# Attention scores from two float32r products: keys stacked as high and low parts on 128 rows, queries copied to both halves

## The chip, the cores and the metric

The kernel runs on one core of one Trainium2 chip. The metric is the device time of one execution in microseconds (us). TensorE (PE) multiplies, VectorE (DVE) and ScalarE (ACT) do element-wise work, GpSimd (POOL) helps, and SyncE (SP) issues nearly all DMAs from one queue, in order.

## The reference, cut to what matters

One backbone layer over 512 latent and 256 context tokens of width 2048: adaLN-modulated RMSNorm, one input projection split into attention heads and RWKV-7 heads, an output projection, and SwiGLU. The part that the change touches is the windowed attention:

```
q, k = axial_rope(q), axial_rope(k)                 # 16 query heads, 4 key heads, HEAD_DIM 64
s_band = where(valid, einsum(q * 64**-0.5, k in a band of up to 384 tokens), -1e30)
s_ctx  = einsum(q * 64**-0.5, k_ctx)                # 256 context keys
p      = sink_softmax(concat(s_band, s_ctx), sink)
out    = einsum(p, concat(v_band, v_ctx))
```

The other part is the modulation vector, `mod = silu(c) @ ada_w + ada_b`: 64 of its 96 columns of 128 values are made as row sums on DVE (`ada_rows`), two halves each.

## The kernel before

All tensors are held with the channels on the 128 partitions. A float32 weight product is made as three float32r products (`mm3`): the weight is split into a rounded high part (`whi`, ACT) and a rest (`wlo`, DVE), and so is the activation. The stages in order of time are:

- **Preparation of the tokens and keys** (0 to 168 us): RMSNorm, the first modulation columns, and the key tiles `psk[0..1]`, `pskc` and the first two query tiles `psk[2..3]`.
- **Query tiles 2 and 3 of head group 0, then the values** (168 to 228 us). `rotate` applies the rotary embedding on DVE (a shuffle, two products, a sum). The values need four 512 KB weights (L421). Sixteen of the modulation row sums are emitted here, four for each weight (L420).
- **Attention** (228 to 570 us): 32 units `(g, b, i)`: head group, block of 128 queries, and pair of heads. The pair's two heads lie on partitions 0 to 63 and 64 to 127 of `qT[g, i]`, their keys on the same halves of `kT[g]`. `scores(u)` makes, for either head `e`, the scores against 512 keys (first and last block) or 640 keys, in pieces of 256, 256 and 128 columns (L472), and adds the band's masks by a bf16 product with an identity (L475). Then DVE takes the maximum (L485), ACT the exponentials (L490, L492), and DVE divides (L497). `transposed(u)` turns the probabilities on PE (L506, L512) and ACT copies them out of the single PSUM buffer `pt` (L507, L513); `values_out` multiplies with the values (L524).
- **Preparation of the eight RWKV pairs** (570 to about 1020 us): key, value and partly `r` tiles, decays and the factors that are spilled to DRAM.
- **RWKV chunks and output projection** (to about 1820 us), then **SwiGLU** (to the end).

In the attention stage PE's order is written out by hand (`manual_schedule`); the other engines' order comes from a list scheduler that works with modelled times, and each engine and the SP queue then runs its list in order. In iteration `u` PE gets the transposes of unit `u` and the scores of unit `u + 2`, and between them pieces of "fill": the remaining query tiles of group 1, four `r` tiles and the two LoRA tiles (`fill_stream`, 188 steps of three products). After a finished tile the fill is withheld for `HOLD` = 3 calls. Each iteration also emits modulation row sums:

```
for u in range(len(units)):
    advance(rows, 3 if u % 2 else 2)
```

A row sum loads 512 KB into one of four buffers `raw` of pool `wp`, which the weights of `split_weight` use too, and is one pass of DVE over 128x1024 (L171). The names that the change touches are `kT`, `qT`, `q0`, `scores`, `rsqrt_newton`'s tiles, `NPR` (the number of probability buffers `pr`, two for a unit) and `rows`.

## Time and profile before

| | us |
|---|---|
| median of 3 runs | 3333.99 (3332.64 to 3337.11) |
| profiled execution: its time | 3328.19 |
| profiled execution: its span | 3326.4 |
| mean granted TensorE clock | 0.974 of 2.4 GHz |
| PE busy | 3161.6 (95%) |
| DVE busy | 1743.5 (52%) |
| ACT busy | 1161.0 (35%) |

Busy PE time is not PE at its peak: products overlap, and only the distance from one start to the next tells what one costs. An idle time is listed with what ended it ("<-DVE pr L497": the DVE instruction of line 497 that wrote `pr`).

### The profile page before, as it was taken

What the parts mean: (1) busy time and instruction counts of PE and PEld (TensorE: products, weight loads), DVE (VectorE), ACT (ScalarE), POOL (GpSimd) and SP (SyncE); (2) the same over time, 40 slices, a digit from 0 to 9 for tenths busy, and PEclk for the clock granted to TensorE, in tenths of its full rate; (3) what the DMA queues carried; (4) which work ended last, traced back from release to release, by engine and by line L of the source; (5) the groups of instructions that cost most, each with busy time, mean ns of one, the idle gap of its engine ahead of it and who ended that gap; (6) DMA issues with size and microseconds to landing.
All of it is one profiled execution on the core that took longest, in us unless ns stands there. A gap on an engine that the chain in (4) does not pass through costs nothing.

```text
span 3326.4 us, 49781 instructions
## 1 busy us (share of the span) xinstructions
PE 3161.6 (95%) x19840; PEld 2468.2 (74%) x19840; DVE 1743.5 (52%) x2906; ACT 1161.0 (35%) x2007; POOL 561.0 (17%) x597
## 2 busy tenths in 40 slices
PE   8989889989998999999997999999999999999997
PEld 4576557767775777777776788888888888888886
DVE  3377764576656777888885653323333232323233
ACT  4213333444344555555553422212221222112221
POOL 0000000253427344434433100000000000000011
PEclk9999999999999999999998999999999999999999
DMA  9675552354536345455465353322232223222232
GB/s 326 242 237 173 182 165 77 108 144 125 138 102 187 105 125 156 141 151 152 127 189 174 128 193 125 103 85 94 92 107 89 95 92 107 94 88 92 93 111 79
DMA packets 270920, 448.41 MB, mean 135 GB/s; under 512 B 109408, under 2 KB 156768, under 8 KB 270688
## 3 DMA queue, kind: packets, MB, share of 16 engines
q1 hardware_dynamic: 270688, 445.22, 42.9%
q8 instruction: 157, 2.57, 0.3%
q14 instruction: 75, 0.61, 0.1%
HBM read 383.52 MB, written 61.60 MB: 134 GB/s over the span
## 4 chain that ended last, share of the span: by engine, by line
PE 60%; DVE 4%; DMA 2%; POOL 1%; issue 1%; SPq 1%; ACT 0%; DVEq 0%; ACTq 0%; POOLq 0%
PE ps_u L114 10%; PE ps_u L113 10%; PE ps_u L110 10%; PE ps_d L113 5%; PE ps_d L110 5%; PE ps_d L114 5%; PE ps_x L852 2%; PE ps_m L982 2%; PE ps_y L863 2%; PE ps_op L110 2%; PE ps_i L901 2%; PE ps_op L114 1%; PE ps_op L113 1%; PE ps_i L907 1%; PE ps_w L971 1%; PE ps_c L1008 1%
## 5 line engine op out<-in xcount | busy, mean ns | idle before, releaser
L1264 ACT ACTIVATE whi<-raw 128x1024 fp32r<-128x1024 f32 (+1 forms) x240 | 275.0, 1146 | 1109.0 <-PE ps_u L113 603.8
L1265 DVE TENSOR_TENSOR wlo<-raw,whi 128x1024 fp32r<-128x1024 f32 (+1 forms) x238 | 317.9, 1336 | 501.2 <-ACT whi L1264 500.5
L114 PE MATMUL ps_u<-ahi,wlo 128*128 128x512 f32 x1408 | 563.0, 400 | 1.2 <-DVE wlo L1265 1.2
L113 PE MATMUL ps_u<-alo,whi 128*128 128x512 f32 x1408 | 556.1, 395 | 0.9 <-DVE alo L1280 0.9
L110 PE MATMUL ps_u<-ahi,whi 128*128 128x512 f32 x1408 | 552.6, 393 | 4.6 <-ACT whi L1264 2.9
L113 PEld LDWEIGHTS ps_u<-alo,whi 128*128 128x128 f32 x1408 | 265.0, 188 | 70.5 <-DVE alo L1280 1.6
L110 PEld LDWEIGHTS ps_u<-ahi,whi 128*128 128x128 f32 x1408 | 265.2, 188 | 69.1 <-ACT whi L1264 4.2
L114 PEld LDWEIGHTS ps_u<-ahi,wlo 128*128 128x128 f32 x1408 | 265.1, 188 | 62.9 <-DVE wlo L1265 2.0
L205 POOL TENSOR_TENSOR sq<-sq 128x512 f32<-128x512 f32 x22 | 40.8, 1855 | 1428.1 <-ACT sq L201 1427.8
L113 PE MATMUL ps_d<-glo,whi 128*128 128x512 f32 x704 | 273.3, 389 | 0.0
L110 PE MATMUL ps_d<-ghi,whi 128*128 128x512 f32 x704 | 273.3, 389 | 0.0
L114 PE MATMUL ps_d<-ghi,wlo 128*128 128x512 f32 x704 | 273.2, 389 | 0.0
L110 PE MATMUL ps_z<-hhi,whi 128*128 128x512 f32 x544 | 230.7, 424 | 7.6 <-DVE r__3128 L309 4.0
L114 PE MATMUL ps_z<-hhi,wlo 128*128 128x512 f32 x544 | 220.1, 405 | 16.8 <-DVE wlo L106 16.8
L113 PE MATMUL ps_z<-lo,whi 128*128 128x512 f32 x544 | 219.5, 403 | 0.0
L171 DVE SCALAR_TENSOR_TENSOR arow<-arow,siluB 128x1024 f32<-128x1024 f32 x128 | 156.4, 1223 | 116.2 <-DMA arow<-ada_t 115.6
L1315 DVE SCALAR_TENSOR_TENSOR x<-ps_d,modT,x 128x512 f32<-128x512 f32 x64 | 48.1, 751 | 299.8 <-PE ps_d L114 299.8
L893 POOL TENSOR_TENSOR bdB<-XY,mk 64x256 f16<-64x256 f32 x192 | 149.3, 777 | 171.7 <-DVE XY L854 156.0
L106 DVE TENSOR_TENSOR wlo<-raw,whi 128x1024 fp32r<-128x1024 f32 x80 | 106.3, 1329 | 92.3 <-ACT whi L105 92.1
L110 PEld LDWEIGHTS ps_d<-ghi,whi 128*128 128x128 f32 x704 | 132.1, 188 | 27.6
L114 PEld LDWEIGHTS ps_d<-ghi,wlo 128*128 128x128 f32 x704 | 132.1, 188 | 27.5
L113 PEld LDWEIGHTS ps_d<-glo,whi 128*128 128x128 f32 x704 | 132.1, 188 | 27.4
(624 smaller groups left out, 5770.4 us busy)
## 6 DMA issues: line engine op xcount, KB each, us to landing
raw<-w SPq DMA_DIRECT2D x176, 512.0 KB, 3.5
arow<-ada_t SPq DMA_DIRECT2D x128, 512.0 KB, 4.2
raw<-w SPq DMA_DIRECT2D x64, 704.0 KB, 4.1
raw<-w_in SPq DMA_DIRECT2D x72, 512.0 KB, 4.1
ada<-ada_w SPq DMA_DIRECT2D x64, 512.0 KB, 6.7
p1d<-pr SPq DMA_DIRECT2D x64, 256.0 KB, 2.8
XB<-bkd SPq DMA_DIRECT2D x96, 128.0 KB, 3.2
pr<-p1d SPq DMA_DIRECT2D x48, 256.0 KB, 3.2
```

The costliest lines, as they stand in the source:

```text
L106: nc.vector.tensor_tensor(lo, raw, hi.bitcast(F32), op=ALU.subtract)
L110: mm = nc.tensor.matmul(ps, lhsT=whi, rhs=hhi, start=first, stop=False)
L113: nc.tensor.matmul(ps, lhsT=whi, rhs=hlo, start=False, stop=False)
L114: nc.tensor.matmul(ps, lhsT=wlo, rhs=hhi, start=False, stop=last)
L171: nc.vector.scalar_tensor_tensor(a, a, 1.0, siluB[:, 1024 * h:1024 * h + 1024], op0=ALU.mult, op1=ALU.mult, accum_out=macc[:, j - 32, h:h ...
L852: nc.tensor.matmul(px[:, u, :], lhsT=AL[:, d, s_ + u, :], rhs=XB[:, d, s_ + u, :], start=True, stop=True)
L863: nc.tensor.matmul(py[m, u, :n], lhsT=XB[:, d, u, 64 * h:64 * h + P][:, m], rhs=GRz[h][:, d, u, :n], start=True, stop=True)
L893: nc.gpsimd.tensor_tensor(diag(B[l], h, d), ab[h][:, d], lm(l, h, d), op=ALU.mult)
L901: nc.tensor.matmul(ps[:, d, u, :], lhsT=lhs[:, d, u, :], rhs=rhs[:, d, u, :], start=True, stop=True)
L982: nc.tensor.matmul(pm[m, u, :n], lhsT=WT[e][h][:, d, u, m], rhs=YB[h][:, d, u, :n], start=True, stop=True)
L1264: nc.scalar.activation(hi[:, :n], raw[:, :n], AF.Copy)
L1265: eng.tensor_tensor(lo[:, :n], raw[:, :n], hi[:, :n].bitcast(F32), op=ALU.subtract)
```

## The change

The scores are no longer float32 products over the 64 partitions of a head. For each of the four key heads (`2 * g + e`) the keys' high part lies on partitions 0 to 63 of `KS[:, 2 * g + e]` and the keys' rest on partitions 64 to 127. The query block is copied to both halves and split into `qh` and `ql`. Two float32r products over 128 rows, `qh` and `ql` against `KS`, give the sum of all four part products. To move data between partitions, rotated keys go to DRAM (`kd_`) and come back in eight loads of 64 partitions, and rotated queries go to DRAM (`qd`) in sixteen stores and come back in two loads of 64 partitions for each unit. Keys are split once (ACT copies, DVE subtractions); queries are split for each unit (`queries`), one unit ahead of its scores. A `stage` tile takes the place of `q0` and later of the `at` pool's four `q1` tiles. `NPR` falls from 5 to 4, `rsqrt_newton`'s two scratch tiles are shared, the catch-up of the fill moves from `u == 14` to `u == 13`, and 32 of the 80 row sums of the attention loop are emitted in the preparation of the RWKV pairs.

```diff
--- before.py
+++ after.py
@@ -51,7 +51,7 @@
 NX, NM = 3, 2
 NPI, NPF = 3, 2
 POOL_LEVELS = (3, 4)
-NPR = 5
+NPR = 4
 HOLD, NE = 3, 5
 
 ORDER = "FBABAC"
@@ -115,9 +115,9 @@
 
     def rsqrt_newton(pool, x, n, lnscale, lnbias, tag):
 
-        v = pool.tile([P, n], F32, tag=tag + "v", name="rs_v", bufs=1)
+        v = pool.tile([P, T], F32, tag="rsv", name="rs_v", bufs=1)[:, :n]
         nc.scalar.activation(v, x, AF.Identity, bias=lnbias, scale=lnscale)
-        l = pool.tile([P, n], F32, tag=tag + "l", name="rs_l", bufs=1)
+        l = pool.tile([P, T], F32, tag="rsl", name="rs_l", bufs=1)[:, :n]
         nc.scalar.activation(l, v, AF.Ln)
         y = pool.tile([P, n], F32, tag=tag + "y", name="rs_y", bufs=1)
         nc.scalar.activation(y, l, AF.Exp, scale=-0.5)
@@ -224,6 +224,8 @@
     bvd = [dram.tile([P, T], F32, name=f"bvd{p}") for p in range(NP_)]
     p1d = [dram.tile([KT, P, T], F32, name=f"p1d{f}") for f in range(4)]
     gtd = [dram.tile([P, T], F32, name=f"gtd{p}") for p in range(NP_)]
+    kd_ = [dram.tile([P, TA], F32, name=f"kd{g}") for g in range(2)]
+    qd = [[dram.tile([4, 64, 2, P], F32, name=f"qd{g}_{i}") for i in range(4)] for g in range(2)]
 
     siluT = const.tile([P, KT, 32], F32, name="siluT")
     sel = const.tile([P, 2], F32, name="sel")
@@ -322,7 +324,8 @@
         kvx = ExitStack()
         kv = kvx.enter_context(tc.tile_pool(name="kv", bufs=1, reuse_waits="tile"))
         rope = kv.tile([P, 2, T], F32, name="rope")
-        kT = [kv.tile([P, TA], F32, name=f"kT{g}") for g in range(2)]
+
+        KS = kv.tile([P, 4, TA], F32R, name="KS")
         vt = kv.tile([P, 6, 256], F32, name="vt")
         shuf = [(i + 16) % 32 for i in range(32)]
 
@@ -333,13 +336,18 @@
             nc.vector.tensor_tensor(sh, sh, rope[:, 1, :], op=ALU.mult)
             nc.vector.tensor_tensor(dst, dst, sh, op=ALU.add)
 
-        qT = {}
-        q0 = zp.tile([P, 4, T], F32, tag="q0", name="q0")
+
+        stage = zp.tile([P, 4 * T], F32, tag="q0", name="stage")
         wad = []
 
+        def q_done(g, i, ps, dst):
+            rotate(ps, dst)
+            for e in range(2):
+                nc.sync.dma_start(qd[g][i][:, :, e, :].rearrange("b r x -> r b x"),
+                                  dst[64 * e:64 * e + 64].rearrange("r (b x) -> r b x", b=4))
+
         def q_tile(g, i, dst):
-            qT[g, i] = dst
-            return z_gen(T_Q + 4 * g + i, False, lambda ps, o, n: rotate(ps, qT[g, i]))
+            return z_gen(T_Q + 4 * g + i, False, lambda ps, o, n: q_done(g, i, ps, dst))
 
 
         with tc.tile_pool(name="st", bufs=2, reuse_waits="tile") as st, tc.tile_pool(name="ps_st", bufs=1, space=PSUM, reuse_waits="tile") as ps_st, \
@@ -406,13 +414,24 @@
                         w_h, w_l = (w_[:, (4 * g + i) * P:(4 * g + i + 1) * P] for w_ in w_q)
                         mm3(psk[2 + g], w_h, w_l, hhi[:, k, :], hlo[k], k == 0, k == KT - 1)
             for g in range(2):
-                rotate(psk[g], kT[g][:, C:])
-                nc.scalar.activation(kT[g][:, :C], pskc[g], AF.Copy)
+                kt = stage[:, TA * g:TA * g + TA]
+                rotate(psk[g], kt[:, C:])
+                nc.scalar.activation(kt[:, :C], pskc[g], AF.Copy)
+                nc.sync.dma_start(kd_[g], kt)
+                for e in range(2):
+                    for h in range(2):
+                        nc.sync.dma_start(KS[64 * h:64 * h + 64, 2 * g + e, :].bitcast(F32), kd_[g][64 * e:64 * e + 64])
             for i in range(2):
-                qT[0, i] = q0[:, i, :]
-                rotate(psk[2 + i], qT[0, i])
+                q_done(0, i, psk[2 + i], st.tile([P, T], F32, tag="sq", name="q0", bufs=3))
             for i in range(2, 4):
-                run(q_tile(0, i, q0[:, i, :]))
+                run(q_tile(0, i, st.tile([P, T], F32, tag="sq", name="q0", bufs=3)))
+            for a in range(4):
+                up, dn = KS[0:64, a, :], KS[64:128, a, :]
+                nc.scalar.activation(up, up.bitcast(F32), AF.Copy)
+                for c0, c1 in ((0, T), (T, TA)):
+                    kh = st.tile([P, T], F32R, tag="sq", name="kh", bufs=3)[64:128, :c1 - c0]
+                    nc.scalar.activation(kh, dn[:, c0:c1].bitcast(F32), AF.Copy)
+                    nc.vector.tensor_tensor(dn[:, c0:c1], dn[:, c0:c1].bitcast(F32), kh.bitcast(F32), op=ALU.subtract)
 
             psv = [ps_st.tile([P, 512], F32, tag=f"b{b}", name=f"ps_v{b}")[:, :256] for b in range(6)]
             rows = ada_rows(wp, "raw", [P, 1024], 4, range(32, 80))
@@ -450,10 +469,27 @@
                 lo_b, hi_b = max(0, b - 1), min(3, b + 1)
                 return lo_b, hi_b - lo_b + 1
 
+            qs = {}
+
+            def queries(u):
+
+                g, b, i = units[u]
+                q = at.tile([P, 2, P], F32, tag="q", name="q_", bufs=3)
+                for h in range(2):
+                    nc.sync.dma_start(q[64 * h:64 * h + 64], qd[g][i][b])
+                qh = at.tile([P, 2, P], F32R, tag="qh", name="qh", bufs=2)
+                ql = at.tile([P, 2, P], F32R, tag="ql", name="ql", bufs=2)
+                nc.scalar.activation(qh, q, AF.Copy)
+                nc.vector.tensor_tensor(ql, q, qh.bitcast(F32), op=ALU.subtract)
+                qs[u] = qh, ql
+
             def scores(u):
 
 
                 g, b, i = units[u]
+                if u + 1 < len(units):
+                    queries(u + 1)
+                qq = qs.pop(u)
                 lo_b, nb = band(b)
                 n = (nb + 2) * P
                 masks = {}
@@ -465,12 +501,12 @@
                 for e in range(2):
                     o = n * e
                     cuts = sorted({o, o + 256, o + n} | {x for x in range(0, 3 * T, T) if o < x < o + n})
-                    r = slice(64 * e, 64 * e + 64)
                     for c0, c1 in sorted(zip(cuts, cuts[1:]), key=lambda c: e != (c[0] // T == 1)):
                         here = [m for m in masks if c0 <= o + m < c1]
                         kc = c0 - o if c0 - o < 256 else C + lo_b * P + c0 - o - 256
-                        nc.tensor.matmul(sc2[:, c0:c1], lhsT=qT[g, i][r, b * P:(b + 1) * P],
-                                         rhs=kT[g][r, kc:kc + c1 - c0], start=True, stop=not here)
+                        for x, q in enumerate(qq):
+                            nc.tensor.matmul(sc2[:, c0:c1], lhsT=q[:, e, :], rhs=KS[:, 2 * g + e, kc:kc + c1 - c0],
+                                             start=(x == 0), stop=(x == 1 and not here))
                         for m in here:
                             nc.tensor.matmul(sc2[:, o + m:o + m + P], lhsT=id_bf, rhs=mbf[:, masks[m]:masks[m] + P],
                                              start=False, stop=(m == here[-1]))
@@ -530,7 +566,7 @@
 
             def fill_stream():
                 for i in range(4):
-                    yield from q_tile(1, i, at.tile([P, T], F32, name=f"q1{i}", bufs=1))
+                    yield from q_tile(1, i, stage[:, T * i:T * i + T])
                 for p in range(4):
                     yield from r_tile(p)
                 wad.append(zp.tile([P, 4 * T], F32, tag="q0", name="wad"))
@@ -560,12 +596,13 @@
                     next(st_z, None)
 
             with tc.manual_schedule(engines={mybir.EngineType.PE}):
+                queries(0)
                 run(scores(0))
                 run(scores(1))
                 fill_all(NE)
                 for u in range(len(units)):
-                    advance(rows, 3 if u % 2 else 2)
-                    if u == 14:
+                    advance(rows, 2 if u % 2 else 1)
+                    if u == 13:
 
                         fill_all(int(todo))
                         todo, hold = 0.0, 0
@@ -584,7 +621,6 @@
                         if k < 2:
                             fill(FILL_T[2 * k + 1])
                 values_out(*units[-1][:2])
-                run(rows)
                 run(st_z)
         kvx.close()
         yp = ysx.enter_context(tc.tile_pool(name="yp", bufs=2, side="right", reuse_waits="tile"))
@@ -655,6 +691,7 @@
                         nc.sync.dma_start(vtd[p][h, :, half::2, :], vsv[64 * half:64 * half + 64, :, h, :])
 
                 for d in range(2):
+                    advance(rows, 2 if p < 7 else 9)
 
                     pw = lora_mm(lu, 0, wd, d)
                     sig = pp.tile([P, NC_, 65], F32, tag="t", name="sig", bufs=5)
```

## Rows read from the trace of the kernel before

**Rows 1.** Windows of the attention stage: length, engines busy, PEclk, DMA share, GB/s.

```profile
228.00:281.00 53.00, 41.27 (x181) 28.57 (x182) 38.36 (x80) 16.58 (x40) 0.00 (x0) 0.87 0.62 207
281.00:327.00 46.00, 41.86 (x191) 27.90 (x193) 35.27 (x72) 16.38 (x36) 0.00 (x0) 0.93 0.59 189
...
362.00:405.00 43.00, 36.61 (x157) 24.20 (x158) 30.01 (x67) 15.37 (x37) 0.00 (x0) 0.88 0.57 178
405.00:449.00 44.00, 39.10 (x171) 25.11 (x171) 29.21 (x59) 15.31 (x35) 0.00 (x0) 0.92 0.49 160
449.00:496.00 47.00, 38.81 (x180) 25.50 (x176) 30.51 (x58) 17.60 (x37) 0.00 (x0) 0.93 0.55 175
496.00:533.00 37.00, 36.42 (x194) 25.19 (x195) 22.51 (x52) 15.09 (x36) 0.00 (x0) 1.00 0.30 93
```

**Rows 2.** PE by line, 228 to 570 us: busy, mean ns, idle before.

```profile
L472 PE MATMUL ps_s<-kT,q 64*128 64x256 f32 (+1 forms) x320 | 90.2, 395 | 0.0
L110 PE MATMUL ps_z<-hhi,whi 128*128 128x512 f32 x160 | 74.9, 468 | 7.1 <-DVE r__3128 L309 4.0 <-DVE r__2929 L309 1.9 <-DVE wad L309 1.3
...
L506 PE MATMUL ps_pt<-cf,pr 128*128 128x128 f32 x256 | 41.7, 288 | 26.7 <-DVE pr L497 21.1 <-ACT PT L507 3.5 <-ACT ao L527 1.6
L524 PE MATMUL ps_pv<-PT,vt 128*64 128x512 f32 x144 | 32.7, 598 | 1.9 <-ACT PT L513 1.9
...
L512 PE MATMUL ps_pt<-cf,pr 128*128 128x128 f32 x32 | 6.2, 276 | 2.9 <-ACT PT L507 2.9
```

**Rows 3.** Timeline of PE, one head, 640 keys: start us, length us, instruction.

```profile
332.15 1.13 PE L472 MATMUL ps_s<-kT,q 64*128 64x256 f32 x4
333.21 0.23 PE L475 MATMUL ps_s<-mbf,id_bf 128*128 128x128 bf16 x1
333.37 0.48 PE L472 MATMUL ps_s<-kT,q 64*128 64x128 f32 x2
333.78 0.23 PE L475 MATMUL ps_s<-mbf,id_bf 128*128 128x128 bf16 x1
```

**Rows 4.** Timeline of PE, two neighbouring float32r products of the value stage.

```profile
194.33 0.28 PE L431 MATMUL ps_v<-wlo,chi 128*128 128x256 f32 x1
194.45 0.28 PE L432 MATMUL ps_v<-whi,lo 128*128 128x256 f32 x1
```

**Rows 5.** DVE by line, 228 to 570 us.

```profile
L171 DVE SCALAR_TENSOR_TENSOR arow<-arow,siluB 128x1024 f32<-128x1024 f32 x77 | 94.2, 1223 | 57.2 <-DMA arow<-ada_t 56.8
...
L106 DVE TENSOR_TENSOR wlo<-raw,whi 128x1024 fp32r<-128x1024 f32 x20 | 24.4, 1219 | 9.1 <-ACT whi L105 9.0
```

**Rows 6.** ACT by line, 228 to 570 us.

```profile
L513 ACT COPY PT<-ps_pt 128x256 f32<-128x256 f32 x16 | 6.0, 373 | 23.6 <-PE ps_pt L512 23.6
```

**Rows 7.** Timelines of DVE and PE around the first units.

```profile
220.54 1.22 DVE L171 SCALAR_TENSOR_TENSOR arow<-arow,siluB 128x1024 f32<-128x1024 f32 x1 [3.25 <-DMA arow<-ada_t]
...
239.53 1.22 DVE L485 TENSOR_REDUCE sm<-ps_s 128x2 f32<-128x1024 f32 x1
...
248.43 1.11 PE L506 MATMUL ps_pt<-cf,pr 128*128 128x128 f32 x4 [11.73 <-DVE pr L497]
```

**Rows 8.** Timeline of PE: transposes in steady work and after a wait.

```profile
333.85 0.61 PE L506 MATMUL ps_pt<-cf,pr 128*128 128x128 f32 x4
...
394.39 1.09 PE L506 MATMUL ps_pt<-cf,pr 128*128 128x128 f32 x4 [6.23 <-DVE pr L497]
```

**Rows 9.** Waits of the SP queue, 168 to 570 us: total, times, longest.

```profile
SPq L170 <- DVE arow L171: 115.9, 47, 5.9
```

**Rows 10.** DMA issues, 228 to 570 us: KB each, us to landing.

```profile
lu<-lora_up SPq DMA_DIRECT2D x2, 128.0 KB, 3.0
```

**Rows 11.** Timeline of DVE, value stage: the last value weight's rest.

```profile
216.06 1.23 DVE L106 TENSOR_TENSOR wlo<-raw,whi 128x1024 fp32r<-128x1024 f32 x1 [0.54 <-ACT whi L105]
```

**Rows 12.** Waits in the RWKV pairs' preparation, 570 to 1020 us.

```profile
DVE cum L669 <- ACT sig L667: 50.0, 8, 7.7
...
PE ps_b L724 <- DVE wad L722: 17.0, 4, 4.3
```

## Prediction, made before the changed kernel ran

> **What bounds the kernel now.** I read the page first: PE is busy 95% of the span, so the question is what PE does in the stretch that the change touches. The windows of the attention stage come next [rows 1]. They show a stage that is almost PE-bound but not quite: PE is busy 78 to 98% of a stretch, its granted clock averages 0.87 to 0.93 in five of them, and DVE is busy around 70%. In the last listed stretch, where the DMAs carry half as much (0.30 against 0.49 to 0.62), PE is nearly gapless at full clock.
>
> Then the PE instructions grouped by line [rows 2]. The scores are the largest group but for the fill's three, 90.2 us of overlapping busy time, and the idle time ahead of all groups adds to 38.6 us (26.7 + 7.1 + 1.9 + 2.9): 21.1 for divided probabilities (`pr`, DVE), 9.9 for ACT to empty a transposed or value tile, 7.2 for DVE to empty a fill tile. The reader should see two kinds of time: PE's own work, and waits for a softmax chain on DVE and ACT.
>
> The stage lasts from 228 to 570, 342 us. Five windows are below full clock; at two levels, 1.2 and 2.4 GHz, a mean clock c over a length L means 2(1 - c)L at the lower one: 13.8 + 6.4 + 10.3 + 7.0 + 6.6 = 44 us [rows 1]. Some of that is idle. The work in the rest ran at half speed, which lost between (44 - 38.6)/2 = 3 and 22 us; I take 15. PE's work at full clock is then 342 - 38.6 - 15, near 288 us.
>
> **The scores' products.** A head with 640 keys takes 1.06 us for its two pieces of 256 columns and 0.41 us for the one of 128, masks apart; a float32 product shows as two records [rows 3]. A float32r product over 128 rows and 256 columns, with a weight load of its own, starts 0.12 us after its neighbour [rows 4]. Two for each piece make 4 x 0.12 = 0.48 instead of 1.06. For 128 columns no row shows float32r. Below, half of 0.12; above, one float32 record of that width, 0.41/2 = 0.205; I take 0.12, since the nearest row has the same weight load. So a head with 640 keys falls from 1.47 to 0.72, saving 0.75 us, one with 512 keys from 1.06 to 0.48, saving 0.58. There are 16 units of either kind and two heads in each: 32 x 0.75 + 32 x 0.58 = 42.6 us of PE. The 64 products of 128 columns put the bounds at 37 and 46. The Trainium skill, "TensorE: Matmul & The Clock Gate", section "Back-to-back issue gap", has about 56 ns for an isolated product of 128 columns at full clock; by it the 64 products would cost 4 us less and the saving would be 46.7, but no row here shows it.
>
> Masks, transposes, values and fill stay. The order on PE is the same, so all of this lies on the path wherever PE isn't already waiting.
>
> **The waits in the stage.** First, the start: DVE runs nine row sums between 220.5 and 239.5 us, 2.1 us each with what lies between them, before the first maximum, and PE then stands 11.7 us for the first probabilities [rows 7]. In the loop as changed, units 0 to 3 emit 6 row sums instead of 10. Four fewer take some 8 us from the chain, but PE arrives 2 x 2 x 0.58 = 2.3 us sooner: the wait shrinks by about 5. Between, one row sum is 1.22 us of DVE plus 57.2/77 = 0.74 us of waiting for its load, and DVE stands in order meanwhile, with maxima and divisions queued behind [rows 5]. 32 fewer free 32 x 1.96 = 63 us of DVE. I let the later waits for `pr` and for a fill tile (9.4 + 7.2) shrink by 4. Against it, the second transpose of a unit waits for ACT to empty `pt`, and the scores between the two are its cover; that cover is 0.6 to 0.75 us thinner, so these 9.9 us grow by perhaps 4. Idle falls from 38.6 to about 33.6, and I give back 2 of the 15 us of half clock in proportion.
>
> The queries' split adds 32 copies on ACT, 0.37 us each by a copy of 256 columns [rows 6], 12 us, and 32 subtractions on DVE, a quarter of 1.22, 10 us [rows 5]. Both fit beside PE's work: DVE is busy 186 of the 260 us listed [rows 1], so at most some 245 of the stage; that becomes 245 - 39 + 10 = 216 against some 246 of PE. Uncovered, they would cost 22 us. `NPR` of 4 costs nothing: two units' buffers are still there, and those of unit u are released by its last transposes, ahead of the exponentials of u + 2; uncovered, it would add one division, about a microsecond a unit.
>
> So the stage goes from 342 to 342 - 42.6 - 5 - 2, near 292 us. In the bad case, waits take back half of the products' saving; in the good one, DVE's waits and the half clock vanish (below).
>
> **Before the stage.** The keys' eight loads, two stores and eight query stores of group 0 enter SP's queue beside the value weights; a load back must wait for its store, and what stands behind it on SP (row sums, a value weight) waits too, some 3 us by the landing time of a small load [rows 10]. On DVE the keys' rests add four times 768 columns on 64 partitions, by L106's rate 0.9 us each, 3.7 us; ACT copies twice that many but is mostly idle. What is late next is the last value weight: its rest starts at 216.06 and is ready near 217.2 [rows 11], while PE's fourth quarter of the values starts about 3 x 72 x 0.12 = 26 us after the first, near 220. So 3 us of slack against 4 to 7 us of delay: I charge 2 us, between 0 and 8. The shared `rsqrt_newton` tiles cost nothing, because the second use comes after 16 further squares on ACT; without that cover, one activation, under 1 us.
>
> **After the stage.** 32 row sums go into the preparation of the pairs, 4 a pair. There DVE has holes, 50.0 us before the scans alone, but also a burst that ends in PE's wait for `wad` of about 4.2 us a pair [rows 12]. In a hole a row sum costs nothing; in the burst it costs 1.22 to 1.96 us of PE. Its load takes one of four `raw` buffers, and everything behind it on SP (spills, next weights) waits if the buffer is late; weights are fetched several ahead, which covers that. If all fell into the burst: 32 x 1.96 = 63 us. Its loads depend on nothing recent, so a scheduler can put most into holes: I take a tenth, 6 us, between 0 and 63.
>
> **Sum**, on the profiled execution's own 3328.19 (span 3326.4): -42.6 (scores) - 5 (idle) - 2 (clock) + 2 (values) + 6 (row sums moved) = -41.6, so 3286.6. The median of the runs lies 5.8 above the profiled time, so 3292; I say 3291.
>
> **Rivals.**
>
> *Waits take the place of the work.* PE needs a unit's probabilities about a unit and a quarter after its scores. A wait of 6.23 us [rows 8] shows that the chain is already late at times, and the transposes right after it took 1.09 instead of 0.61 us, the lower clock. If idle and half clock grow by 22 us instead of falling by 7, the sum is -12.6: 3321. For it: a chain as long as before against a shorter unit. Against: two fifths of its row sums are gone. Chance 0.20.
>
> *DVE was the real brake.* If all 28.3 us of PE's waits for DVE and 10 of the half clock go, the sum is -42.6 - 38.3 + 8 = -73: 3261. For it: the gapless last stretch [rows 1]. Against: waits for ACT stay, and PE comes sooner. Chance 0.09.
>
> *The row sums land in the burst of the preparation.* 63 us there instead of 6: the sum is +15, 3349, slower. It decides from some 48 us, 1.5 us for each of the 32. For it: they are emitted right ahead of the decays, in that burst. Against: the holes. Chance 0.05.
>
> *Queries come late.* A load on SP stands behind a row sum that waits 2.5 us for its buffer on average, 5.9 at most [rows 9]; then 3.0 us to land [rows 10], 0.7 us of ACT and DVE. One unit ahead, that is 6 to 10 us against 292/32 = 9 of lead. The Trainium skill, "DMA: Bandwidth & Descriptors", section "Rules for kernel authors", says that two transfers to disjoint halves of the partitions serialize; no row here shows it. With two landings in a row, 12.6 at worst, 24 of 32 units would wait 3.6 us: +86, 3379, slower. Against: three `q` buffers let the loads run two units earlier. Chance 0.04.
>
> *The change does not do it:* the pairs of float32r products run no faster than one float32 product. Then only the side terms stay, about 3335. Against: [rows 4]. Chance 0.03.
>
> **How the numbers follow.** The likeliest case has 0.59; its own range, from the bounds of its terms, is 3270 to 3310. About 0.2% (6.7 us) is what a measurement of this kernel can tell from no change. Faster: 0.59 + most of 0.20 + 0.09, 0.84; same: the rest of the second case and the last one, 0.07; slower: 0.09. The range 3261 to 3324 leaves out part of the fastest case, part of the second and both slow ones.
>
> **What the profile would show.** Scores as float32r over 128 rows, 0.12 us apart, for 128 columns too; the stage near 290 us; the first wait for `pr` near 7 us; more and shorter waits for `pt`; no wait of PE for `ql`; the moved row sums in DVE's holes before the scans, and PE's wait for `wad` unchanged. The prediction fails if PE's waits for `pr` grow, if PE waits for `qh` or `ql` in most units, or if the wait ahead of L724 grows by 2 us or more a pair.

## The result and the profile after

| | before | after |
|---|---|---|
| median, us | 3334.0 (3332.6 to 3337.1, 4 runs) | 3293.4 (3289.5 to 3296.4, 4 runs) |
| profiled execution: span, us | 3326.4 | 3287.8 |

The ratio is 0.9877, with a 95% interval of 0.9862 to 0.9893. The forecast was 3291, and the total came out within 2.4 us of it. The stages under that total did not all come out as forecast; errors of either sign cancel in it. A stage is counted here from PE's first product of one kind to its first product of the next kind, in the profiled executions:

| stage, us | before | after | difference | forecast |
|---|---|---|---|---|
| up to the values | 193.6 | 196.6 | +3.0 | |
| values | 34.7 | 40.2 | +5.5 | +2 with the row above |
| attention | 341.8 | 299.8 | -42.0 | -49.6 |
| of it PE at work | 303.2 | 254.4 | -48.8 | -44.6 |
| of it PE waiting | 38.6 | 45.4 | +6.8 | -5 |
| preparation of the pairs | 466.0 | 460.7 | -5.3 | +6 |
| RWKV chunks, output projection, SwiGLU | 2290.3 | 2290.5 | +0.2 | 0 |
| sum | | | -38.6 | -41.6 |

The windows of the kernel after, in the attention stage, some left out (length; then PE, PEld, DVE, ACT, POOL busy; PEclk; DMA share; GB/s), answers to [rows 1]:

```profile
236.00:284.00 48.00, 33.47 (x183) 27.70 (x182) 33.42 (x74) 18.84 (x46) 0.00 (x0) 0.86 0.54 176
...
357.00:394.00 37.00, 30.08 (x157) 21.57 (x158) 24.80 (x55) 15.99 (x39) 0.00 (x0) 0.95 0.49 155
394.00:429.00 35.00, 31.29 (x169) 23.41 (x167) 24.87 (x57) 16.58 (x37) 0.00 (x0) 0.95 0.41 132
...
467.00:499.00 32.00, 30.11 (x191) 23.57 (x191) 20.33 (x48) 17.01 (x41) 0.00 (x0) 1.00 0.21 67
...
236.80:536.60 299.80, 254.43 (x1426) 193.88 (x1426) 196.80 (x439) 136.14 (x308) 0.00 (x0) 0.94 0.43 139
```

The last line is the whole stage. PE is at work 85% of it (254.43 of 299.80); before it was 89%. So PE bounds the stage less than it did. From 467 to 499 us, where the DMAs carry little (0.21), PE is again nearly gapless, at full clock. A low DMA share is not what decides, though: a stretch of the kernel before that [rows 1] leaves out had 96% and full clock at a share of 0.56:

```profile
327.00:362.00 35.00, 33.63 (x163) 21.05 (x161) 26.77 (x58) 14.97 (x32) 0.00 (x0) 1.00 0.56 173
```

PE by line, from 236 to 532 us (busy, mean ns, idle before), answers to [rows 2]:

```profile
L110 PE MATMUL ps_z<-hhi,whi 128*128 128x512 f32 x160 | 75.4, 471 | 11.1 <-DVE r__3387 L311 3.9 <-DVE r__3163 L311 2.8 <-DVE r__2926 L311 2.7
...
L508 PE MATMUL ps_s<-KS,qh 128*128 128x256 f32 (+1 forms) x160 | 45.8, 304 | 1.1 <-ACT pr L528 0.9 <-ACT vt L453 0.3
L508 PE MATMUL ps_s<-KS,ql 128*128 128x256 f32 (+1 forms) x160 | 41.6, 283 | 0.0
L542 PE MATMUL ps_pt<-cf,pr 128*128 128x128 f32 x256 | 40.6, 282 | 26.0 <-DVE pr L533 18.0 <-ACT PT L543 6.8 <-ACT PT L549 0.9
L560 PE MATMUL ps_pv<-PT,vt 128*64 128x512 f32 x144 | 34.2, 621 | 3.6 <-ACT PT L549 3.6
...
L548 PE MATMUL ps_pt<-cf,pr 128*128 128x128 f32 x32 | 6.6, 290 | 3.4 <-ACT PT L543 3.3
```

No wait names `qh` or `ql`. The waits for `pr` fell only from 21.1 to 18.0. Those for ACT rose from 9.9 to 15.8 (6.8 + 0.9 + 0.9 + 0.3 + 3.6 + 3.3), those for a fill tile from 7.2 to 11.3.

PE's timeline of one head with 640 keys, in steady work (start, length), answers to [rows 3]:

```profile
295.88 0.28 PE L508 MATMUL ps_s<-KS,qh 128*128 128x256 f32 x1
296.00 0.28 PE L508 MATMUL ps_s<-KS,ql 128*128 128x256 f32 x1
296.12 0.28 PE L508 MATMUL ps_s<-KS,qh 128*128 128x256 f32 x1
296.24 0.28 PE L508 MATMUL ps_s<-KS,ql 128*128 128x256 f32 x1
296.37 0.23 PE L511 MATMUL ps_s<-mbf,id_bf 128*128 128x128 bf16 x1
296.40 0.30 PE L508 MATMUL ps_s<-KS,qh 128*128 128x128 f32 x1
296.55 0.27 PE L508 MATMUL ps_s<-KS,ql 128*128 128x128 f32 x1
296.66 0.23 PE L511 MATMUL ps_s<-mbf,id_bf 128*128 128x128 bf16 x1
296.70 0.48 PE L110 MATMUL ps_z<-hhi,whi 128*128 128x512 f32 x1
```

The products with 256 columns stand 0.12 us apart, those with 128 take 0.15 and 0.11. From its first product to the instruction behind it the head takes 0.82 us. Before, it took 333.85 - 332.15 = 1.70 [rows 3, 8].

The first units, on DVE and PE, answers to [rows 7]:

```profile
240.33 1.22 DVE L171 SCALAR_TENSOR_TENSOR arow<-arow,siluB 128x1024 f32<-128x1024 f32 x1
...
241.48 1.22 DVE L521 TENSOR_REDUCE sm<-ps_s 128x2 f32<-128x1024 f32 x1
...
247.29 1.23 DVE L171 SCALAR_TENSOR_TENSOR arow<-arow,siluB 128x1024 f32<-128x1024 f32 x1 [2.72 <-DMA arow<-ada_t]
...
251.96 1.23 DVE L171 SCALAR_TENSOR_TENSOR arow<-arow,siluB 128x1024 f32<-128x1024 f32 x1 [1.78 <-DMA arow<-ada_t]
...
254.04 1.12 PE L542 MATMUL ps_pt<-cf,pr 128*128 128x128 f32 x4 [10.82 <-DVE pr L533]
```

The first maximum still stands behind row sums. Three more stand between it and the division that PE waits for, two of them with load waits of 2.72 and 1.78 us; the shown ones are those two.

In the preparation (waits from 536 to 990 us: total, times, longest), the row of `wad` in [rows 12] has become:

```profile
PE ps_z L114 <- DVE wlo L106: 23.3, 5, 5.5
...
PE ps_b L761 <- DVE wad L759: 7.0, 4, 2.3
```

PE's waits for `wad` fell by 10.0 us, and those for weights' rests, 15.8 us in the whole preparation of before, rose by 7.5. All waits of PE together hardly changed (39.5 to 38.7 us); what fell is PE at work, from 426.5 to 422.0 us, at a mean clock of 0.95 and then 0.96.

### The profile page after: what moved, and what is told of

Same layout as the page of the kernel before. It is cut to its first block, busy times and chain, and to the rows that moved or that the text cites. A ratio compares the mean times of both kernels' runs of the same rounds, so it can differ in the third digit from the quotient of the medians.

```text
span 3287.8 us, 50103 instructions
## 1 busy us (share of the span) xinstructions
PE 3115.1 (95%) x19840; PEld 2459.3 (75%) x19840; DVE 1763.5 (54%) x2946; ACT 1179.0 (36%) x2051; POOL 550.7 (17%) x597
## 4 chain that ended last, share of the span: by engine, by line
PE 62%; DVE 4%; DMA 1%; issue 1%; POOL 1%; ACT 1%; SPq 0%; DVEq 0%; ACTq 0%; POOLq 0%
PE ps_u L114 10%; PE ps_u L113 10%; PE ps_u L110 10%; PE ps_d L113 5%; PE ps_d L110 5%; PE ps_d L114 5%; PE ps_m L1019 2%; PE ps_x L889 2%; PE ps_y L900 2%; PE ps_op L110 2%; PE ps_i L938 2%; PE ps_op L114 1%; PE ps_op L113 1%; PE ps_w L1008 1%; PE ps_i L944 1%; PE ps_c L1045 1%
## 5 line engine op out<-in xcount | busy, mean ns | idle before, releaser
L205 POOL TENSOR_TENSOR sq<-sq 128x512 f32<-128x512 f32 x22 | 40.2, 1829 | 1435.0 <-ACT sq L201 1434.7
L171 DVE SCALAR_TENSOR_TENSOR arow<-arow,siluB 128x1024 f32<-128x1024 f32 x128 | 164.5, 1287 | 105.2 <-DMA arow<-ada_t 104.9
L1352 DVE SCALAR_TENSOR_TENSOR x<-ps_d,modT,x 128x512 f32<-128x512 f32 x64 | 48.0, 751 | 299.8 <-PE ps_d L114 299.8
```

Of the source, the lines that this page charges most:

```text
L171: nc.vector.scalar_tensor_tensor(a, a, 1.0, siluB[:, 1024 * h:1024 * h + 1024], op0=ALU.mult, op1=ALU.mult, accum_out=macc[:, j - 32, h:h ...
```

## The experiments

Stages are given as in the table above, each from one profiled execution. What such a stage is good for, three comparisons show. Eight kernels that do not differ in the code up to the values start them between 194.8 and 200.7 us. The stages behind the preparation, which no edit touches, took 2283.4 to 2294.6 us. The attention stage of the kernel before took 341.8 us, and those of two small edits that leave the total as it was (ratio 1.0003, at the end of this section) 347.3 and 353.6. So a difference of less than some 10 us in one stage decides nothing by itself, and the ratios to the kernel before, made on the same chip, stand beside it.

### Either half of the change alone

The changed kernel with the 32 row sums back in the attention loop:

```diff
-                    advance(rows, 2 if u % 2 else 1)
+                    advance(rows, 3 if u % 2 else 2)
...
+                run(rows)
...
-                    advance(rows, 2 if p < 7 else 9)
```

> The changed kernel with its 32 moved row sums back in the attention loop (80 there, none in the pairs' preparation). Theory A (row sums in the attention stage brake PE, those in the preparation are free): the stage grows from 300 to about 310 to 315 us, the preparation stays near 461, the total is 3300 to 3310. Theory B (row sums hide in either place, and the 5 us that the preparation lost have another cause): the stage stays within 5 us of 300, the total within 7 us of 3293. Theory C (row sums cost in the preparation): the preparation falls below 455.

The kernel before with only the 32 row sums moved, by the same lines the other way round:

> The kernel before with only the 32 row sums moved to the pairs' preparation. Theory A: the attention stage falls from 342 to about 330, the preparation stays near 466 or falls to 461, the total is 3315 to 3325. Theory B: total within 7 us of 3334. Theory C: preparation at 472 or more and the total at 3334 or above.

The whole attention stage of the first, then of the second, in the windows' columns:

```profile
237.50:573.50 336.00, 266.68 (x1427) 200.95 (x1426) 234.28 (x507) 136.25 (x308) 0.00 (x0) 0.89 0.55 176
```

```profile
227.50:552.50 325.00, 301.05 (x1425) 200.58 (x1425) 190.94 (x409) 126.40 (x278) 0.00 (x0) 0.95 0.36 116
```

PE's waits are the stage less PE's time at work:

| row sums in the loop, products | PE at work | PE waits | stage | median, us | ratio |
|---|---|---|---|---|---|
| 80, old (before) | 303.2 | 38.6 | 341.8 | 3334 | 1 |
| 80, new | 266.7 | 69.3 | 336.0 | 3330.2 | 0.9980 (0.9970 to 0.9991) |
| 48, old | 301.0 | 24.0 | 325.0 | 3305.8 | 0.9904 (0.9883 to 0.9926) |
| 48, new (after) | 254.4 | 45.4 | 299.8 | 3293.4 | 0.9877 (0.9862 to 0.9893) |

With the row sums left in the loop, the new products take 36.5 us of work from PE and give 30.7 of them back as waits. The stage keeps 5.8 us of it, but it starts 9.2 us later (237.5 against 228.3); what counts here is the ratio of the totals, 0.2% or 6 us (3336.0 for the kernel before beside it, 3330.2). With the row sums moved they take 46.6 us and give back 21.4. The stage keeps 25.2, and starts 9.3 us later (236.8 against 227.5). By the totals alone this second step is not quite clear: the intervals of the last two ratios overlap between 0.9883 and 0.9893. The move alone, without any new product, brings 30 us (3336.0 to 3305.8) of the 41.

Both runs went the way of theory A, and both further than it said: the stage grew by 36 us with the row sums back (10 to 15 said) and the total came to 3330.2 (3300 to 3310 said); with the move alone the total came to 3305.8 (3315 to 3325 said). The preparation took 466.1 us with the row sums back in the loop and 460.6 with them moved, as in the kernels before and after (466.0 and 460.7), so the 5 us that it lost come with the move.

The row of PE's waits in the first run shows the place (18.0 us in the kernel after); those for ACT rose as well, from 15.8 to 24.0 us:

```profile
PE ps_pt L542 <- DVE pr L533: 33.7, 8, 14.1
```

The clock adds to it: at 0.89 the stage ran 2 x 0.11 x 336 = 74 us at the lower of its two levels, against 2 x 0.06 x 299.8 = 36 in the kernel after.

### What the products are worth by themselves

One float32 product over the 128 stacked rows instead of two float32r ones, no query split:

```diff
-                qh = at.tile([P, 2, P], F32R, tag="qh", name="qh", bufs=2)
...
-                qs[u] = qh, ql
+                qs[u] = q
...
-                        for x, q in enumerate(qq):
-                            nc.tensor.matmul(sc2[:, c0:c1], lhsT=q[:, e, :], rhs=KS[:, 2 * g + e, kc:kc + c1 - c0],
-                                             start=(x == 0), stop=(x == 1 and not here))
+                        nc.tensor.matmul(sc2[:, c0:c1], lhsT=qq[:, e, :], rhs=KS[:, 2 * g + e, kc:kc + c1 - c0].bitcast(F32),
+                                         start=True, stop=not here)
```

> The changed kernel with one float32 product over the same 128 rows (unsplit queries on both halves against the keys' high and low parts) in place of two float32r ones; all transfers and row sums as in the changed kernel, only the split of the queries is left out. Theory A (the products are the gain): the stage grows by about 43 us, to some 340, the total to about 3335. Rival (the gain comes from fewer row sums and shorter waits, the products lie under waits): the stage grows by less than 20 us, the total stays under 3315.

It took 3303.2 us (ratio 0.9898, 0.9882 to 0.9915), with a stage of 320.2: 280.2 of work, 40.0 of waits. The stage grew by 20.4 us, half of theory A's 43 and just beyond the rival's bound, and the total stayed under the rival's 3315. The waits fell by only 5.4, though, so the rival's reason does not hold: it is the work itself that grew by only 25.8. PE's timeline of one head with 640 keys in it:

```profile
332.84 1.03 PE L503 MATMUL ps_s<-KS,q__2517 128*128 128x256 f32 x4
333.71 0.22 PE L506 MATMUL ps_s<-mbf,id_bf 128*128 128x128 bf16 x1
333.76 0.44 PE L503 MATMUL ps_s<-KS,q__2517 128*128 128x128 f32 x2
334.04 0.22 PE L506 MATMUL ps_s<-mbf,id_bf 128*128 128x128 bf16 x1
334.07 0.48 PE L110 MATMUL ps_z<-hhi,whi 128*128 128x512 f32 x1
```

This head takes 1.23 us, where the float32 product over 64 rows took 1.70. By PE's timelines, the median over the heads that PE ran without a wait is 1.68, 1.23 and 0.84 us for 640 keys (64 rows; 128 rows; pair of float32r) and 1.10, 0.89 and 0.52 for 512. So the products' saving is 32 x 0.84 + 32 x 0.58 = 45.4 us of PE, and nearly half of it, 32 x 0.45 + 32 x 0.21 = 21.1, comes with the 128 rows.

The other way, the changed kernel without the `ql` products:

```diff
-                        for x, q in enumerate(qq):
+                        for x, q in ((1, qq[0]),):
...
-                                             start=(x == 0), stop=(x == 1 and not here))
+                                             start=True, stop=not here)
```

> The changed kernel with the products of the queries' low part left out (the scores lack that part); the split is still made. 160 products at 0.12 us. Theory A (the stage is still bound by PE): the stage falls by 15 to 19 us, the total to about 3275. Rival (the softmax chain now bounds the stage): it falls by less than 8 us.

```profile
237.80:536.00 298.20, 239.65 (x1265) 177.83 (x1265) 197.48 (x441) 135.69 (x308) 0.00 (x0) 0.91 0.47 141
```

PE lost 254.4 - 239.7 = 14.8 us of work, and its waits grew by 13.2 (to 58.6): the stage is 1.6 us shorter. The median, 3286.0, is 7.4 below that of the kernel after, and the intervals of the two ratios (0.9831 to 0.9860 here) just miss each other. So the rival holds: the stage hardly gets shorter when PE's work does. In the other direction PE's work still sets its length, since 25.8 us more of it made the stage 20.4 longer in the run above. The change has brought the stage to about the point where the softmax chain takes over from PE.

### All row sums out of the loop

The 80 row sums of the loop go to the preparation; and the same with the single float32 product over 128 rows:

```diff
                 for u in range(len(units)):
-                    advance(rows, 2 if u % 2 else 1)
...
-                    advance(rows, 2 if p < 7 else 9)
+                    advance(rows, 5 if p < 7 else 9)
```

> The changed kernel with no row sum in the attention loop (16 in the value stage, 80 in the pairs' preparation). Theory F (row sums between the steps of the softmax chain bound the stage, not PE's products): the stage falls from 300 to about 275 us, where PE's own work (some 250) and its waits for ACT (15) bound it, and the first wait for pr falls from 10.8 to about 5; the preparation grows by 0 to 25 us. Rival (the waits for ACT and for fill tiles bound it): the stage stays above 290.

> All 80 row sums of the attention loop stand in the pairs' preparation, as in the run without row sums in the loop; the scores are one float32 product over the 128 stacked rows again and the queries are not split (keys' parts still stacked: the same sum but for the queries' rounding). Theory A (with the row sums gone PE is the bound, so the product pairs are worth their full 43 us): the attention stage grows from 262.4 to 300 to 308 us, PE's waits stay near 19 us, the time is near 3326. Theory B (even without row sums the softmax chain sets the pace): the stage grows by less than 20 us, to at most 282, PE's waits fall below 10 us, the time is near 3300.

The stage of either, pairs of products first:

```profile
238.60:501.00 262.40, 243.27 (x1426) 186.63 (x1425) 146.22 (x345) 136.60 (x308) 0.00 (x0) 0.99 0.22 67
```

```profile
238.20:511.30 273.10, 263.68 (x1422) 199.25 (x1421) 140.92 (x315) 125.74 (x277) 0.00 (x0) 0.99 0.22 65
```

Without row sums the stage falls from 299.8 to 262.4 us, PE's waits from 45.4 to 19.1, and the clock is 0.99. That is theory F's case, and further than its 275 us. The same PE work, 254.4 us before the 48 were taken out, takes 243.3. The second run's stage was expected at 300 to 308 us and took 273.1. The mistake was to price the float32 product over 128 rows like the one over 64: the work fell by 20.4 us when the pairs came in, which is the 24.3 that the heads give for that half (45.4 - 21.1), to within the scatter. All the numbers of theory B came true (10.7 us more, 9.4 us of waits, 3296.7), but not its reason: PE never waited for `pr` in the second run and was at work 97% of the stage, so PE's work did bound the stage there.

The totals moved less: 3285.6 (0.9854, 0.9840 to 0.9869) and 3296.7 (0.9880, 0.9857 to 0.9903), because the preparation went from 460.7 to 495.1 and 494.9, beyond the 25 us that theory F allowed. The next three runs move other numbers of row sums.

Without the 16 row sums beside the values, these going to the preparation; and with none in either place:

```diff
             for q in range(4):
-                advance(rows, 4)
...
-                    advance(rows, 2 if p < 7 else 9)
+                    advance(rows, 3 if p < 7 else 9)
```

> The changed kernel with the 16 row sums of the value stage in the pairs' preparation as well (48 there, 48 in the attention loop). Theory D (the scores start 8.5 us later because row sums share DVE, buffers and SP's queue with the keys' and queries' transfers): the first scores return from 236.8 to about 230 us, the preparation stays within 3 us of 461, the total falls to about 3287. Rival (the transfers and splits of the keys delay the stage by themselves): the first scores stay at 235 to 237.

> The changed kernel with all 96 row sums in the pairs' preparation, 12 a pair. If row sums are free there up to DVE's holes (some 140 us of 461 without them), the total falls to 3265 to 3275: the first scores near 230, the stage near 275, the preparation grown by 5 to 10. If the holes are full at 64 or 80, the preparation grows by 1.3 us for each further row sum, 20 us or more, and the total is 3285 or above.

The 80 spread over five places of a pair:

```diff
+                advance(rows, 2)
...
+                advance(rows, 2)
...
+                advance(rows, 2)
...
-                    advance(rows, 5 if p < 7 else 9)
+                    advance(rows, 2 if p < 7 else 9)
```

> All 80 row sums of the attention loop in the pairs' preparation as in the run without row sums in the loop, but spread over five places of a pair, two at each, instead of five at one place twice. Theory A (they cost there because five in a row fill the four load buffers and stand in one place of DVE's order): the preparation falls from 495.1 to 470 to 480 us, the attention stage stays at 262, the time is 3265 to 3272. Theory B (DVE has only some 35 free places in the preparation, wherever they are put): the preparation stays at 488 or more, the time at 3280 or more.

| row sums beside values, in the loop, in preparation | values | attention | preparation | median, us | ratio |
|---|---|---|---|---|---|
| 16, 80, 0 (before) | 34.7 | 341.8 | 466.0 | 3334.0 | 1 |
| 16, 48, 32 (after) | 40.2 | 299.8 | 460.7 | 3293.4 | 0.9877 |
| 0, 48, 48 | 34.6 | 296.0 | 477.8 | 3297.8 | 0.9889 (0.9874 to 0.9904) |
| 16, 0, 80 | 37.9 | 262.4 | 495.1 | 3285.6 | 0.9854 (0.9840 to 0.9869) |
| 16, 0, 80 spread | 39.0 | 271.6 | 494.1 | 3289.9 | 0.9864 (0.9840 to 0.9888) |
| 0, 0, 96 | 34.5 | 264.2 | 504.0 | 3287.7 | 0.9862 (0.9836 to 0.9888) |

The first 32 cost the preparation nothing; the next 48 cost it 34.4 us, 0.72 each, and free 37.4 in the loop, 0.78 each. The run with 48 there does not fit one price: its 16 more cost 17.1 us. By it theory D is half right: the first scores did come back to 230.6 us, but the preparation did not stay within 3 us of 461, and the total did not fall to 3287. With all 96 the preparation grew by 43.3 us and the total stayed above 3285: that is the second of that run's two cases, at 0.68 us for each of the 64 instead of 1.3.

Spreading them did not help: the preparation stayed at 494.1, and the wait changed its place. PE's waits in the whole preparation of the kernel with 80 in one place, then spread:

```profile
PE ps_z L114 <- DVE wlo L106: 44.6, 10, 7.8
...
PE ps_b L760 <- DVE wad L758: 5.9, 4, 2.3
```

```profile
PE ps_z L114 <- DVE wlo L106: 32.7, 9, 5.5
PE ps_b L763 <- DVE wad L761: 14.1, 4, 5.4
```

The spread kernel's attention stage is the longer one by 9.2 us (271.6 against 262.4), although no row sum is emitted in its loop. The list scheduler moved four of the preparation's row sums into it, and DVE stood 8.1 us for their loads (DVE by line, 233.8 to 505.4 us):

```profile
L171 DVE SCALAR_TENSOR_TENSOR arow<-arow,siluB 128x1024 f32<-128x1024 f32 x4 | 4.9, 1226 | 8.1 <-DMA arow<-ada_t 8.1
```

So theory B holds for the preparation: it has room for about a third of the row sums. The kernel with 80 moved has the lowest median of those that compute all of it, but its interval overlaps that of the kernel after, so a better version is not shown.

The values are gapless without row sums; this is their window (0 row sums beside them), and below it the one of the kernel after:

```profile
196.00:230.60 34.60, 34.60 (x290) 34.56 (x290) 20.12 (x33) 10.53 (x19) 0.00 (x0) 1.00 0.55 170
```

```profile
196.60:236.80 40.20, 37.73 (x289) 36.51 (x290) 33.50 (x54) 10.56 (x19) 0.00 (x0) 0.96 0.91 298
```

With the row sums' loads, the keys' and the queries' transfers and the weights' in one stretch, the DMA share is 0.91. PE waits 2.5 us, and the clock falls to 0.96.

### Load or pass?

The changed kernel, with the loop's 48 row sums on a resident vector instead of a loaded one:

```diff
+                idle = j < 80 and 16 <= 2 * (j - 32) + h < 64
...
-                nc.sync.dma_start(a, ada_t[j - 32, h])
+                if not idle:
+                    nc.sync.dma_start(a, ada_t[j - 32, h])
```

> The changed kernel; the 48 row sums of the attention loop are computed on a resident vector and their loads are left out, so those 48 half columns have other values. Theory A (DVE stands in order for the loads, and that is most of what a row sum costs the softmax chain): of 299.8 us the stage loses some 34.9 us of load waits less what they already hid behind, so it falls to 270 to 282; the time is near 3270. Theory B (the 1.22 us passes between maxima and divisions are the cost, whatever they wait for): 48 x 1.22 us stay, the stage falls by less than 10 us, to 290 or more.

The stage took 285.4 us, between the two expectations, and the time was 3274.4 (0.9812, 0.9788 to 0.9835):

```profile
237.00:522.40 285.40, 252.11 (x1427) 193.65 (x1426) 192.15 (x433) 135.94 (x308) 0.00 (x0) 0.95 0.21 65
```

In the trace of the kernel after, the loop's row sums stood as follows (DVE by line, 236 to 532 us):

```profile
L171 DVE SCALAR_TENSOR_TENSOR arow<-arow,siluB 128x1024 f32<-128x1024 f32 x45 | 55.0, 1223 | 34.9 <-DMA arow<-ada_t 34.9
```

Of the 37.4 us that these row sums cost the stage, 14.4 go with their loads and 23.0 with their passes (285.4 - 262.4), each to within the scatter of such a stage. The DMA share is the same with the passes and without them (0.21 and 0.22), so lighter transfers do not explain the 23.0. In the 14.4, DVE's waiting and the DMAs' lighter load (0.43 before) are not told apart. As they are less than half of the 34.9 us of waits, a good part of those waits must have lain where nothing was held up by them.

### The small edits

`NPR` = 4 with the shared scratch tiles of `rsqrt_newton`, and `NPR` = 4 alone, each in the kernel before:

```diff
-NPR = 5
+NPR = 4
...
-        v = pool.tile([P, n], F32, tag=tag + "v", name="rs_v", bufs=1)
+        v = pool.tile([P, T], F32, tag="rsv", name="rs_v", bufs=1)[:, :n]
```

> The kernel before with only the two space savers: NPR of 4 and the shared tiles of rsqrt_newton. As predicted they cost nothing: total within 4 us of 3336, attention stage within 3 us of 342. Rival: the shared tiles delay the keys by 1.5 to 3 us (the values start at 195 to 197 instead of 193.6), or NPR of 4 adds 5 us or more to the stage.

> The kernel before with NPR 4 alone. Theory A (two units' buffers are enough): stage 342 us within 5, first value product at 193.6 within 1, time within 4 us of before. Theory B (the 12 us by which the stage was longer in the run with shared scratch tiles and NPR 4 come from NPR): stage 350 us or more, PE's waits for pr up by 5 us or more, time 6 to 10 us above before.

Both ratios are 1.0003 (0.9990 to 1.0015), so the two edits cost nothing that the totals show. The stages were 353.6 and 347.3 us, and the values of the first run started at 196.0, as its rival said. The second stage lies between the two theories' bounds. As the ratios show no change, what the 12 and 6 us of single executions are is left open.

## Why the total was right, point by point

**The products: right, a little too small.** The step "saving 42.6 us of PE" measured 45.4 by the distances of the heads, inside its bounds of 37 and 46. The 128-column product, which no row showed, was taken at 0.12 and takes about that (0.15 and 0.11). The Trainium skill, "TensorE: Matmul & The Clock Gate", section "Back-to-back issue gap", gives about 81 ns as the sustained spacing at 128 columns; here such products stood 0.15 and 0.11 us apart, which is longer. What the step did not see is that float32r is only half of the saving; the other half is that the operands fill 128 rows.

**The half clock: about right.** Forecast 2 us less; by the mean clock of 0.94 in either kernel the stretch at the lower level went from 2 x 0.06 x 341.8 = 41 us to 36, which is at most 2.5 us of lost work. A clock given to two digits leaves some 3 us open at either end.

**The idle time: wrong, and this is the step that failed.** "Idle falls from 38.6 to about 33.6" measured 45.4. "The wait shrinks by about 5" at the first unit measured 0.9 (11.73 to 10.82). The forecast took four row sums off the chain. But eight passes for the keys' rests stand on DVE between 203 and 217 us now, the row sums of the values run among and behind them, and the first maximum still waits for row sums. From it to the first transposes it takes 12.6 us (254.04 - 241.48), against 8.9 before [rows 7]. Three row sums stand in that stretch in either kernel, so the move took none off here. DVE stood 4.5 us for their loads (2.72 + 1.78) where it stood 1.5 before, and two splits of queries (0.41 us each) came in. The two of before with load waits:

```profile
244.60 1.23 DVE L171 SCALAR_TENSOR_TENSOR arow<-arow,siluB 128x1024 f32<-128x1024 f32 x1 [1.11 <-DMA arow<-ada_t]
...
246.35 1.23 DVE L171 SCALAR_TENSOR_TENSOR arow<-arow,siluB 128x1024 f32<-128x1024 f32 x1 [0.43 <-DMA arow<-ada_t]
```

Where the products did not change, the same move did bring the wait down, to 8.5: two row sums stood there, neither with a load wait. In the run with no row sum in the loop it is 1.87 us, and in the one whose loop loads none 3.34:

```profile
246.91 0.66 PE L542 MATMUL ps_pt<-cf,pr 128*128 128x128 f32 x4 [1.87 <-DVE pr L533]
```

```profile
246.77 0.65 PE L544 MATMUL ps_pt<-cf,pr 128*128 128x128 f32 x4 [3.34 <-DVE pr L535]
```

In neither does a row sum stand between the first maximum and these transposes, and the stretch takes 5.9 us (246.91 - 241.02) and 6.0 (246.77 - 240.82). So what kept the first wait long is the row sums between the steps of the first unit's softmax, with the waits for their loads. The later waits for `pr` fell by 2.2 us (9.4 to 7.2). The waits for ACT grew by 5.9 where 4 was said, and those for a fill tile grew by 4.1 where they were to shrink. The sign named as failure, growing waits for `pr`, did not show (21.1 to 18.0): the growth lay in the other two. Why the waits for ACT and for a fill tile grew as much as they did was not tried by itself; with no row sum in the loop they are 9.5 and 6.4 us. One reading of the forecast was wrong without effect: the listed windows of [rows 1] last 270 us, not 260, so DVE's share of the stage comes to some 236 us and not 245 (225.9 in the stage's own window).

**What the move of the row sums is worth: the forecast had it at a few microseconds of waits.** The two-by-two table shows it as the larger part of the gain. The sum was right because it put both edits into one kernel: PE's saving is there, and the moved row sums kept 24 us of it from becoming waits (69.3 to 45.4). The forecast's attribution, 42.6 of 41.6 us to the products, is not what either edit does alone.

**Before the stage: too small.** +2 with bounds of 0 and 8 measured +8.5. The mechanism was the right one, weights for the values that come late among the new transfers, and taking the row sums out of that stretch removes the 5.5 us of it. The other 3.0, ahead of the values, are a step that the forecast put at nothing. They are smaller than the scatter of one execution, but come back on average: the ten kernels with the keys' and queries' transfers start the values at 194.8 to 200.7 us, 197.6 in the mean, the four without them at 192.8 to 196.0, 194.2 in the mean. What makes them is not shown.

**After the stage: wrong sign.** +6, from nothing up to 63, measured -5.3. The row sums went into the holes, as the main case had it. The wait for `wad` fell by 10.0 instead of staying, and those for weights' rests rose by 7.5. That some of the row sums would have to cost something was not needed. The 5.3 us lie almost all in PE at work (426.5 to 422.0), with the clock at 0.95 and then 0.96; why the clock rose is not shown.

The three errors, +11.8 (waits), +6.5 (before the stage) and -11.3 (after it), and the -4.2 of PE's work, leave 2.8 of a sum of 41.6 us (+0.2 is in stages not forecast to move). That they cancel so closely is luck: no step of the forecast says why the waits should cost what the preparation gives back.

**The rivals.** *Waits take the place of the work* is what happens if the row sums stay (69.3 us of waits); with the move it came in part. *DVE was the real brake* holds in the weaker form that DVE's row sums were it: without them the stage takes 262.4 us. But the time that this frees is spent again in the preparation, so 3261 was not in reach by it. *The burst* did not come with 32. With 80 the preparation did grow, by 34.4 us, but as waits for weights' rests (44.6 us) and not for `wad` (5.9). *Queries come late* did not occur: no wait of PE names them; ACT stood 6.92 us for the first block, ahead of the stage, and PE's first scores did not wait for it. The rule of the Trainium skill that stands beside that rival ("DMA: Bandwidth & Descriptors", section "Rules for kernel authors") could not be weighed, since no run loads the queries in one transfer.

## What to carry to other kernels

When one edit shortens an engine's work and another thins the chain that this engine waits for, forecast the two-by-two table: here the shorter work alone gave 0.2%, the thinner chain alone 1.0%, and both 1.2% (the last two intervals overlap). Work put between the steps of a dependent chain on an in-order engine can cost the chain part of its pass and part of its load wait (here 0.78 us for each row sum, whose pass takes 1.22 us and whose load the engine stood 0.78 us for in the mean), even where that engine is busy only two thirds of the time; and a stretch that takes such work in for nothing does so up to a point (32 here), so count its holes before moving the rest.

## What the runs showed of the hardware

- A float32 product over 64 rows cost PE more than one over 128 rows with the same columns: a head of 640 keys took 1.68 us and 1.23 us, of 512 keys 1.10 and 0.89. The two pieces of 256 columns took 1.06 us up to the mask with 64 rows [rows 3] and 0.87 with 128 (333.71 - 332.84). Part of it lies at the change to and from the masks' product: the next piece started 0.16 us after the mask's start with 64 rows and 0.05 with 128. Why is not shown.
- The row sum's pass over 128x1024 took 1.22 us in the attention stage, where POOL is idle, and 1.51 us in a stretch of the preparation where POOL is busy 154.9 of 410 us. DVE by line of the kernel after, 570 to 980 us:

```profile
L171 DVE SCALAR_TENSOR_TENSOR arow<-arow,siluB 128x1024 f32<-128x1024 f32 x28 | 42.3, 1512 | 11.5 <-DMA arow<-ada_t 11.5
```

That POOL is the reason was not tried.

- Where PE waited more, its clock was lower, and its work longer: the same instructions of the attention stage were 266.7 us of work at a mean clock of 0.89, 254.4 at 0.94 and 243.3 at 0.99 (waits of 69.3, 45.4 and 19.1 us).
